# End keys and their transposes ahead, and key products on VectorE, in a gated linear attention

## The chip, the core and the metric

The program runs on one core of a Trainium2 chip. A core has five engines with queues of their own that run in order: TensorE (PE, matmuls; its weight loads are shown as PEld), VectorE (DVE), ScalarE (ACT), GpSimd (POOL) and SyncE (SP, here only DMA issues). The metric is the device time of one execution in microseconds, as the median of several runs.

## The reference

Two macaron layers of an encoder over 512 tokens and 16 meta tokens, width 1024, in float32. Each layer is half a feed-forward block, a mixer, and half a feed-forward block. The mixer adds a softmax attention and a gated linear attention (GLA) in both directions. The change lies in the GLA, with chunks and a decay `log_a` for each key channel:

```python
bcum = jnp.cumsum(log_a..., axis=3)      # inside a chunk
btot = bcum[:, :, :, -1:, :]
q_dec = qc * jnp.exp(bcum)
k_inv = kc * jnp.exp(-bcum)
k_end = kc * jnp.exp(btot - bcum)
att = jnp.where(mask, einsum('bhnid,bhnjd->bhnij', q_dec, k_inv), 0.0)
o_intra = einsum('bhnij,bhnjv->bhniv', att, vc)
kv_chunk = einsum('bhnjd,bhnjv->bhndv', k_end, vc)
# scan over chunks: S = exp(btot) * S + kv_chunk;  o_inter = q_dec @ S_prev
```

The backward direction is the same on the flipped sequence.

## The kernel before

All activations stand transposed, channels on 128 partitions and 528 tokens (512 and 16 meta tokens) along the row. A weight slab of 128x1024 is loaded by SP, split into a high part on ACT (L238, `whi`) and a low part on DVE (L239, `wlo`), and used in three matmuls per tile by `product` (L404); a projection's accumulator (`mm`) is evicted on DVE by `scaled` (L527) or on ACT (L691).

The GLA of a layer is two calls of `gla_pair` (L699), each for two heads, and each with the directions d = 0 (forward) and d = 1 (backward) in turn. The chunks are of 128 tokens, 4 blocks and the meta tokens. For one direction:

1. PE forms the gates z (L721). ACT takes abs, exp and log (L724 to L726), DVE finishes the log-sigmoid (L727) and scans it along each block (L731, five scans): `c` holds the sums.
2. DVE subtracts each block's middle value (`a`, L739 and L740) and its total (`ct_`, L741 and L742, a copy for the meta tokens). For d = 1 it first forms the reversed sums in `g` (L737).
3. ACT makes four exponentials (L746 to L749, or L752 to L755 for d = 1): for the queries, the keys, the state's queries and the end keys.
4. DVE multiplies the queries (`qp`, L757), POOL the keys (`kp`, L758), DVE the end keys (`ke`, L760). PE transposes the end keys (L764 for the blocks, L765 for the meta tokens), DVE copies them out (L767, L769), and makes the state's queries (L777) and copies the decays of blocks (L778).

After both directions PE forms the chunk states from the transposed end keys (L802), two banks `sm` taking turns; DVE chains them with the decays (L809, L817) and ACT copies the backward halves (L806, L813). The scores of queries and keys (L829), their mask (L832, L833) and the outputs (L837, L838) follow.

The order on each engine is not written out: a scheduler of the framework orders all instructions ahead of time by a priority that follows the order of the code, and fills in instructions of later code where it expects an engine to wait. So matmuls of later projections stand between the gates and the transposes on PE. `tc.high_priority()` lifts the instructions inside it over others that are ready. Tiles come from pools of fixed size by tag (`p` has 7, `t` has 6, the PSUM pairs `ss` 2).

Of the kernel before, what the change touches and what calls it, by code (L numbers as in the profile page):

```python
# [13 lines left out]
AF = mybir.ActivationFunctionType  # L14
ALU = mybir.AluOpType
AX = mybir.AxisListType

P = 128
# [3 lines left out]
META = 16  # L22
T = SEQ + META
# [249 lines left out]
def build(tc, ctx, xt, wts, win, par, w2, const, umask, out):  # L273
    nc = tc.nc
    V, S, G, TE = nc.vector, nc.scalar, nc.gpsimd, nc.tensor
# [30 lines left out]
    def nm(p):  # L306
        count[0] += 1
        return f"{p}{count[0]}"
# [3 lines left out]
    def slot(tag, dtype=F32, n=None):  # L312
        return slots[tag].tile([P, T], dtype, tag=tag, name=nm(tag))[:, : n or live[0]]
# [7 lines left out]
    def pair(second=False):  # L321
        return (slots["s2"] if second else pss).tile([P, 2, 512], F32, tag="s2" if second else "ss", name=nm("ss"))
# [22 lines left out]
    ident = ct[:, C_ID : C_ID + P]  # L345
# [7 lines left out]
    def v2(ap):  # L353
        return ap.rearrange("p (a b) -> p a b", a=2)
# [341 lines left out]
    blocks = [(b, slice(b * P, (b + 1) * P), P) for b in range(NB)]  # L696
    MB = slice(SEQ, T)

    def gla_pair(l, p, lr, w2t, sr, qa, ka, va, n_out):  # L699
# [6 lines left out]
        for hh in range(2):  # L706
            tp = pair()
# [6 lines left out]
        def blk(ap):  # L714
            return ap[:, :SEQ].rearrange("p (b t) -> p b t", b=NB)

        for d in range(2):
            z = pair()
            for i, hs in enumerate(halves):
                c0 = p * 256 + d * P  # L720
                TE.matmul(z[:, i, :HF], w2t[:, c0 : c0 + P], lr[:, hs], start=True, stop=True)  # L721
            a, g, c, ct_ = slot("t"), slot("t"), slot("t"), slot("t")

            S.activation(v2(a), z[:, :, :HF], AF.Abs)  # L724
            S.activation(a, a, AF.Exp, scale=-1.0)
            S.activation(a, a, AF.Ln, bias=1.0)  # L726
            V.scalar_tensor_tensor(v2(g), z[:, :, :HF], 0.0, v2(a), ALU.min, ALU.subtract)  # L727
            ones = ct[:, C_COS + SEQ : C_COS + SEQ + 1]
            for bs in [b[1] for b in blocks] + [MB]:
                n = bs.stop - bs.start  # L730
                V.tensor_tensor_scan(c[:, bs], ones.broadcast_to([P, n]), g[:, bs], 0.0, ALU.mult, ALU.add)  # L731
            mid = blk(c)[:, :, 63:64].broadcast_to([P, NB, P])
            tot = blk(c)[:, :, 127:128].broadcast_to([P, NB, P])
            mm_, mt_ = c[:, T - 1 : T].broadcast_to([P, META]), None
            src = c
            if d == 1:
                V.tensor_tensor(g, c, g, ALU.subtract)  # L737
                src = g
            V.tensor_tensor(blk(a), blk(src), mid, ALU.subtract)  # L739
            V.tensor_tensor(a[:, MB], src[:, MB], mm_, ALU.subtract)  # L740
            V.tensor_tensor(blk(ct_), blk(src), tot, ALU.subtract)  # L741
            V.tensor_copy(ct_[:, MB], a[:, MB])  # L742
            r16 = 1.0 / 16.0
            qp, kp = slot("p"), slot("p")
            if d == 0:
                S.activation(g, a, AF.Exp, scale=-r16)  # L746
                S.activation(a, a, AF.Exp, scale=r16)
                S.activation(c, c, AF.Exp, scale=r16)
                S.activation(ct_, ct_, AF.Exp, scale=-r16)  # L749
                ein, eq, ek, eend = c, a, g, ct_  # L750
            else:
                S.activation(c, a, AF.Exp, scale=-r16)  # L752
                S.activation(a, a, AF.Exp, scale=r16)
                S.activation(ct_, ct_, AF.Exp, scale=-r16)
                S.activation(g, g, AF.Exp, scale=r16)  # L755
                ein, eq, ek, eend = ct_, c, a, g
            V.tensor_tensor(qp[:, :n_out], qa, eq[:, :n_out], ALU.mult)  # L757
            G.tensor_tensor(kp, ka, ek, ALU.mult)  # L758
            ke = slot("p")
            V.tensor_tensor(ke, ka, eend, ALU.mult)  # L760

            tp = pair()
            for b, bs, _ in blocks:
                TE.transpose(tp[:, 0, bs], ke[:, bs], ident)  # L764
            TE.transpose(tp[:META, 1, :P], ke[:, MB], ident)  # L765
            for hh in range(2):
                V.tensor_copy(kt[hh][:, :SEQ].rearrange("p (b k) -> p b k", b=NB)[:, :, d * HD : (d + 1) * HD],  # L767
                              tp[:, 0].rearrange("p (b k) -> p b k", b=NB)[:, :, hh * HD : (hh + 1) * HD])
            V.tensor_copy(ktm[:META, 0:256].rearrange("p (h d k) -> p d h k", d=2, h=2)[:, d],  # L769
                          tp[:META, 1, :P].rearrange("p (h k) -> p h k", h=2))  # L770
            if qin is None:
                qin = [slot("p"), slot("p")]
            e0 = 127 if d == 0 else 0
            for hh in range(2):
                rows = slice(hh * HD, (hh + 1) * HD)
                to = slice(d * HD, (d + 1) * HD)
                V.tensor_tensor(qin[hh][to, :n_out], qa[rows], ein[rows, :n_out], ALU.mult)  # L777
                V.tensor_copy(dec[to, hh, :], blk(ein)[rows, :, e0])  # L778
            prods.append((qp, kp))
# [41 lines left out]
        for b in [3, 2, 1, 0] + [NB] * (n_out == T):  # L821
            bs, n = (MB, META) if b == NB else (blocks[b][1], P)
# [239 lines left out]
    def mixer(l, norm, done, following):  # L1062
# [15 lines left out]
        for p in range(2):  # L1078
            qa = project(x, rs, "i", 0.125, n_out)
            ka = project(x, rs, "i")  # L1080
            va = [project(x, rs, "i") for _ in range(2)]
            gla_pair(l, p, lr, w2t, sr, qa, ka, va, n_out)
# [115 lines left out]
    for l in range(DEPTH):  # L1198
        a, b, c = norms[3 * l : 3 * l + 3]
# [3 lines left out]
        if l < DEPTH - 1:  # L1203
            d = norms[3 * l + 3]
# [71 lines left out]
```

## Time and profile before

| | us |
|---|---|
| median of 3 runs | 2267.22 (2266.92 to 2269.97) |
| the profiled execution | 2263.49 |
| its span, first to last instruction | 2261.6 |
| PE busy | 2204.5 |
| DVE busy | 1527.2 |
| ACT busy | 1218.3 |
| POOL busy | 164.7 |

The four calls of `gla_pair` lie between about 427 and 524 us (layer 0) and between 1569 and 1656 us (layer 1). A row of a timeline reads: start, duration, engine, line and operation, output<-inputs, shapes, count, and in brackets the idle time of the engine just before and who ended it. A row of a wait reads: engine, what waited <- for whom: us in total, times, the longest. A row of windows reads: from:to, length, then the busy time of PE, PEld, DVE, ACT and POOL with the number of instructions, the granted PE clock, the share of the DMA engines and GB/s.

### The profile page before, as it was taken

The numbers are of one execution on the slowest core, as the hardware profiler recorded it, in microseconds if no ns is written. First come the engines' busy times: TensorE is split into PE (matmuls) and PEld (weight loads), VectorE is DVE, ScalarE is ACT, GpSimd is POOL, SyncE is SP. The second block draws the span as 40 slices with busy tenths as digits, with TensorE's granted clock in tenths as the row PEclk, the third lists the DMA queues.
The fourth block names the chain that finished last, engine by engine and source line by source line (L and its number), as shares of the span: only waits on it lengthen the run. The fifth ranks groups of instructions, "written<-read, shape, count | busy, mean of one in ns | idle before, by whom it ended". The sixth has DMA issues, their size and how long they took to land. (4 is left out here: it accounts for less than half of the span.)

```text
span 2261.6 us, 39885 instructions
## 1 busy us (share of the span) xinstructions
PE 2204.5 (97%) x16538; PEld 2102.9 (93%) x16538; DVE 1527.2 (68%) x2397; ACT 1218.3 (54%) x1824; POOL 164.7 (7%) x184
## 2 busy tenths in 40 slices
PE   8999999999999999999979999999999999999998
PEld 8999999989999999999979999998888888989897
DVE  7657567577876666565676565575789767756565
ACT  8536355344784564453565363454557836636354
POOL 1011000000000010101011010100000000101010
PEclk9999999999999999999999999999999999999999
DMA  8778463211113485867658585732121135869661
GB/s 239 188 177 212 134 168 108 75 57 57 48 38 113 124 203 154 197 174 173 180 139 207 139 217 149 178 105 87 56 68 54 47 121 152 215 155 225 156 181 66
DMA packets 87542, 312.85 MB, mean 138 GB/s; under 512 B 9664, under 2 KB 11840, under 8 KB 87360
## 3 DMA queue, kind: packets, MB, share of 16 engines
q1 hardware_dynamic: 60816, 217.67, 28.6%
q0 software_dynamic: 24768, 90.19, 22.5%
q8 instruction: 130, 2.13, 0.4%
q10 hardware_dynamic: 1776, 2.43, 0.3%
q14 instruction: 52, 0.43, 0.1%
HBM read 263.07 MB, written 2.10 MB: 117 GB/s over the span
## 5 line engine op out<-in xcount | busy, mean ns | idle before, releaser
L597 PE MATMUL ss<-xc,whi 128*128 128x264 f32 (+1 forms) x4720 | 865.1, 285 | 16.9 <-ACT whi L238 9.5
L597 PEld LDWEIGHTS ss<-xc,whi 128*128 128x128 f32 x4720 | 734.7, 189 | 19.7 <-ACT whi L238 10.3
L597 PE MATMUL ss<-xc,wlo 128*128 128x264 f32 (+1 forms) x2360 | 671.4, 285 | 5.1 <-DVE wlo L239 5.1
L404 PE MATMUL ss<-g,whi 128*128 128x264 f32 (+1 forms) x2620 | 482.8, 300 | 0.0
L597 PEld LDWEIGHTS ss<-xc,wlo 128*128 128x128 f32 x2360 | 446.8, 189 | 6.4 <-DVE wlo L239 6.3
L404 PEld LDWEIGHTS ss<-g,whi 128*128 128x128 f32 x2620 | 380.6, 188 | 15.7
L404 PE MATMUL mm<-x,whi 128*128 128x264 f32 (+1 forms) x1712 | 385.8, 315 | 0.0
L238 ACT CAST whi<-w 128x1024 fp32r<-128x1024 f32 (+1 forms) x220 | 230.0, 1046 | 266.2 <-PE ss L404 116.1
L239 DVE TENSOR_TENSOR wlo<-w,whi 128x1024 fp32r<-128x1024 f32 (+1 forms) x220 | 266.6, 1218 | 116.1 <-ACT whi L238 114.8
L238 ACT CAST whi<-raw 128x1024 fp32r<-128x1024 f32 x190 | 199.2, 1048 | 260.2 <-PE ss L597 89.8
L239 DVE TENSOR_TENSOR wlo<-raw,whi 128x1024 fp32r<-128x1024 f32 x190 | 232.1, 1222 | 105.8 <-ACT whi L238 104.8
L404 PE MATMUL ss<-g,wlo 128*128 128x264 f32 (+1 forms) x1310 | 302.2, 300 | 0.0
L404 PEld LDWEIGHTS mm<-x,whi 128*128 128x128 f32 x1712 | 281.2, 190 | 15.3 <-DVE x L393 0.2
L404 PE MATMUL mm<-x,wlo 128*128 128x264 f32 (+1 forms) x856 | 265.2, 314 | 0.0
L404 PEld LDWEIGHTS ss<-g,wlo 128*128 128x128 f32 x1310 | 209.2, 188 | 8.3
L239 DVE TENSOR_TENSOR wlo<-s,whi 128x1024 fp32r<-128x1024 f32 x86 | 105.1, 1222 | 95.7 <-ACT whi L238 95.6
L238 ACT CAST whi<-s 128x1024 fp32r<-128x1024 f32 x86 | 90.3, 1050 | 146.9 <-PE ss L597 128.3
L404 PEld LDWEIGHTS mm<-x,wlo 128*128 128x128 f32 x856 | 161.2, 190 | 7.6
L527 DVE SCALAR_TENSOR_TENSOR t<-ss,rs 128x528 f32<-128x528 f32 (+1 forms) x93 | 64.6, 700 | 126.4 <-PE ss L404 126.3
L189 ACT ACTIVATE s<-w 128x1024 f32<-128x1024 f32 x86 | 91.2, 1060 | 81.7 <-DMA w<-win 46.5
L194 POOL DMA_DIRECT2D w<-win x43 | 37.8, 880 | 599.3 <-DVE wlo L239 222.3
L393 DVE TENSOR_TENSOR g<-c,g 128x528 fp32r<-128x528 f32 (+1 forms) x88 | 61.5, 699 | 22.6 <-ACT g L392 22.6
(280 smaller groups left out, 2829.6 us busy)
## 6 DMA issues: line engine op xcount, KB each, us to landing
w<-win SPq DMA_DIRECT2D x218, 512.0 KB, 4.7
raw<-wts SPq DMA_DIRECT2D x190, 512.0 KB, 3.3
w<-win POOLq DMA_DIRECT2D x43, 512.0 KB, 6.8
s<-win POOLq DMA_DIRECT2D x43, 512.0 KB, 6.7
w<-s POOLq DMA_DIRECT2D x43, 512.0 KB, 5.9
s<-w POOLq DMA_DIRECT2D x43, 512.0 KB, 7.0
h<-xt SPq DMA_DIRECT2D x3, 528.0 KB, 7.6
out<-h SPq DMA_DIRECT2D x2, 512.0 KB, 2.9
```

Of the source, the lines that this page charges most:

```text
L189: self.nc.scalar.activation(t, w, AF.Copy, scale=-1.0)
L194: self.nc.gpsimd.dma_start(t, src, accum_op=ALU.add)
L238: nc.scalar.copy(hi[:, cs], w[:, cs])
L239: nc.vector.tensor_tensor(lo[:, cs], w[:, cs], hi[:, cs].bitcast(F32), ALU.subtract)
L393: V.tensor_tensor(lo, src, hi.bitcast(F32), ALU.subtract)
L404: TE.matmul(acc.half[i][:width], lhs, rhs[:, acc.spans[i]], start=first, stop=last)
L527: V.scalar_tensor_tensor(cut(dst[rows]), pv[rows], -0.5 * f, cut(rs[rows]), ALU.mult, ALU.mult)
L597: TE.matmul(acc[:, j], a[:, j, k], b[:, at], start=bool(begin and k == 0 and i == 0), stop=k == len(x) - 1 and i == 2, skip_group_check=no ...
```

## The change

Four edits, in both directions: the end-key chain (subtraction of totals, exponential, product) is written first after the scans and under high priority; the transposes of the end keys are written right behind it; the exponential goes straight into the tile `ke`, which is then multiplied in place; and the product of the keys, `kp`, moves from POOL to DVE. In the forward direction the meta tokens' copy becomes a subtraction. In the backward one, `ct_` (for the state's queries alone) is formed later. No arithmetic changes.

```diff
-            mm_, mt_ = c[:, T - 1 : T].broadcast_to([P, META]), None
+            last = c[:, T - 1 : T].broadcast_to([P, META])
+            r16 = 1.0 / 16.0
+            ke = slot("p")
             src = c
-            if d == 1:
-                V.tensor_tensor(g, c, g, ALU.subtract)
-                src = g
+            with tc.high_priority():
+                if d == 0:
+                    V.tensor_tensor(blk(ct_), blk(c), tot, ALU.subtract)
+                    V.tensor_tensor(ct_[:, MB], c[:, MB], last, ALU.subtract)
+                    S.activation(ke, ct_, AF.Exp, scale=-r16)
+                else:
+                    V.tensor_tensor(g, c, g, ALU.subtract)
+                    S.activation(ke, g, AF.Exp, scale=r16)
+                    src = g
+                V.tensor_tensor(ke, ka, ke, ALU.mult)
+            tp = pair()
+            for b, bs, _ in blocks:
+                TE.transpose(tp[:, 0, bs], ke[:, bs], ident)
+            TE.transpose(tp[:META, 1, :P], ke[:, MB], ident)
             V.tensor_tensor(blk(a), blk(src), mid, ALU.subtract)
-            V.tensor_tensor(a[:, MB], src[:, MB], mm_, ALU.subtract)
-            V.tensor_tensor(blk(ct_), blk(src), tot, ALU.subtract)
-            V.tensor_copy(ct_[:, MB], a[:, MB])
-            r16 = 1.0 / 16.0
+            V.tensor_tensor(a[:, MB], src[:, MB], last, ALU.subtract)
             qp, kp = slot("p"), slot("p")
             if d == 0:
...
-                S.activation(ct_, ct_, AF.Exp, scale=-r16)
-                ein, eq, ek, eend = c, a, g, ct_
+                ein, eq, ek = c, a, g
             else:
+                V.tensor_tensor(blk(ct_), blk(src), tot, ALU.subtract)
+                V.tensor_copy(ct_[:, MB], a[:, MB])
...
-                S.activation(g, g, AF.Exp, scale=r16)
-                ein, eq, ek, eend = ct_, c, a, g
+                ein, eq, ek = ct_, c, a
             V.tensor_tensor(qp[:, :n_out], qa, eq[:, :n_out], ALU.mult)
-            G.tensor_tensor(kp, ka, ek, ALU.mult)
-            ke = slot("p")
-            V.tensor_tensor(ke, ka, eend, ALU.mult)
-
-            tp = pair()
-            for b, bs, _ in blocks:
-                TE.transpose(tp[:, 0, bs], ke[:, bs], ident)
-            TE.transpose(tp[:META, 1, :P], ke[:, MB], ident)
+            V.tensor_tensor(kp, ka, ek, ALU.mult)
```

New lines of the changed kernel that are named below: L740, L741 and L744 the subtractions, L742 and L745 the exponential and L747 the product of the end key, L750 and L751 its transposes, L767 and L768 the products of queries and keys, L770 and L772 the copies out, L780 the state's queries, L781 the decays, L805 the state products, L812 their chain.

What the scheduler makes of it, on DVE in layer 0, first call, forward direction, behind the scans (`t_4917` is `c`, `t_4918` is `ct_`, `t_4915` is `a`; `wlo` is a weight split; L527 evicts a projection):

```order
-L739 TENSOR_TENSOR t_4915<-t_4917 128x512
-L740 TENSOR_TENSOR t_4915<-t_4917 128x16
-L741 TENSOR_TENSOR t_4918<-t_4917 128x512
-L742 COPY t_4918<-t_4915 128x16
+L740 TENSOR_TENSOR t_4918<-t_4917 128x512
+L741 TENSOR_TENSOR t_4918<-t_4917 128x16
 L239 TENSOR_TENSOR wlo_5151<-raw_4779,whi_5150 128x1024
-L778 COPY dec_4890<-t_4917 64x4 x2
-L757 TENSOR_TENSOR p_4932<-i_4654,t_4915 128x528
-L760 TENSOR_TENSOR p_4940<-i_4713,t_4918 128x528
+L747 TENSOR_TENSOR p_4928<-i_4713,p_4928 128x528
+L781 COPY dec_4890<-t_4917 64x4 x2
```

The end-key product stands right behind the weight split; the decay copies and the query product, which stood ahead of it, come after it.

The same queue in the backward direction, before (`t_4961` is `g`, `t_4963` is `ct_`):

```order
L737 TENSOR_TENSOR t_4961<-t_4962,t_4961 128x528
L739 TENSOR_TENSOR t_4960<-t_4961,t_4962 128x512
L741 TENSOR_TENSOR t_4963<-t_4961,t_4962 128x512
L757 TENSOR_TENSOR p_4978<-i_4654,t_4962 128x528
L777 TENSOR_TENSOR p_4951<-i_4654,t_4963 64x528
L760 TENSOR_TENSOR p_4986<-i_4713,t_4961 128x528
```

and now:

```order
L744 TENSOR_TENSOR t_4961<-t_4962,t_4961 128x528
L752 TENSOR_TENSOR t_4960<-t_4961,t_4962 128x512
L747 TENSOR_TENSOR p_4973<-i_4713,p_4973 128x528
L761 TENSOR_TENSOR t_4963<-t_4961,t_4962 128x512
L767 TENSOR_TENSOR p_4985<-i_4654,t_4962 128x528
L768 TENSOR_TENSOR p_4986<-i_4713,t_4960 128x528
L780 TENSOR_TENSOR p_4951<-i_4654,t_4963 64x528
L812 SCALAR_TENSOR_TENSOR q_5001<-q_5001,dec_4890,sm_5010 64x128 x2
```

The end-key product moves ahead of the query product and of the subtraction of totals; the query and key products (L767, L768) now stand behind it and ahead of the first state update (L812).

On PE, the projection matmuls (L404) between the gates and the transposes become fewer. In layer 0 there were 73 and 87 in the first call (forward, backward) and are 66 and 69, and in the second 80 and 91 and are 66 and 81; in layer 1 there were 50 and 97, and 40 and 62, and are 35 and 79, and 40 and 38. Behind the backward transposes of the first call stands now:

```order
L750 MATMUL ss_4977<-const,p_4973 128x128 x4
L751 MATMUL ss_4977<-const,p_4973 16x128
L832 MATMUL ss_5041<-p_4941,p_4942 128x128 x2
L404 MATMUL mm_5267<-x_4202,wlo_4776 128x264
...
L805 MATMUL sm_5006<-k_4895 128x128 x2
L805 MATMUL sm_5010<-q_4893,q_4891 128x128
L805 MATMUL sm_5010<-q_4894,q_4892 128x128
L832 MATMUL ss_5056<-p_4941,p_4942 128x128
L805 MATMUL sm_5016<-q_4893,q_4891 128x128
L805 MATMUL sm_5016<-q_4894,q_4892 128x128
L832 MATMUL ss_5041<-p_4985,p_4986 128x128 x2
```

The scores of the backward direction (from `p_4985` and `p_4986`), which stood beside those of the forward one right behind the transposes, now come after three pairs of state products. SP's queue keeps its order, and POOL's loses the eight products L758 and nothing else.

## The prediction

> **What bounds the kernel now.** I read the page first, then the waits of TensorE (PE), then the timeline of the four passes of the linear attention, engine by engine.
>
> ```profile
> PE 2204.5 (97%) x16538; PEld 2102.9 (93%) x16538; DVE 1527.2 (68%) x2397; ACT 1218.3 (54%) x1824; POOL 164.7 (7%) x184
> PE ss L764 <- DVE p L760: 12.5, 8, 2.1
> PE ss L597 <- ACT whi L238: 9.5, 4, 4.7
> ```
>
> PE is busy for 97% of the span, and the change adds and takes away none of its work. So the end moves only by PE's idle time and by its clock. The largest wait of PE is the one that the change is about: eight times (two layers, two passes, two directions) the transposes of the end keys (L764) wait for the DVE product that makes them (L760), 12.5 us in all. The next row belongs to the feed-forward part, which the change leaves alone. The eight places, with the idle time before each in brackets:
>
> ```profile
> 439.77 0.63 PE L764 MATMUL ss<-const,p 128*128 128x128 f32 x4 [1.46 <-DVE p L760]
> 453.47 0.30 PE L764 MATMUL ss<-const,p 128*128 128x128 f32 x1 [2.13 <-DVE p L760]
> 492.67 0.34 PE L764 MATMUL ss<-const,p 128*128 128x128 f32 x1 [1.83 <-DVE p L760]
> 507.80 0.41 PE L764 MATMUL ss<-const,p 128*128 128x128 f32 x2 [1.49 <-DVE p L760]
> 1581.13 0.41 PE L764 MATMUL ss<-const,p 128*128 128x128 f32 x2 [1.43 <-DVE p L760]
> 1595.25 0.41 PE L764 MATMUL ss<-const,p 128*128 128x128 f32 x2 [1.31 <-DVE p L760]
> 1629.30 0.41 PE L764 MATMUL ss<-const,p 128*128 128x128 f32 x2 [1.11 <-DVE p L760]
> 1642.57 0.41 PE L764 MATMUL ss<-const,p 128*128 128x128 f32 x2 [1.75 <-DVE p L760]
> ```
>
> A wait is the length of a chain (gates, scans, exponentials, product) less the projection matmuls that stand ahead of the transposes on PE and cover it. The change shortens both, so each must be counted.
>
> **The first place, forward direction.** DVE's queue from the end of the scans, with ACT's exponential and POOL's key product beside it:
>
> ```profile
> 433.94 0.69 DVE L739 TENSOR_TENSOR t<-t 128x512 f32<-128x512 f32 x1
> 434.55 0.17 DVE L740 TENSOR_TENSOR t<-t 128x16 f32<-128x16 f32 x1
> ...
> 435.66 1.22 DVE L239 TENSOR_TENSOR wlo<-raw,whi 128x1024 fp32r<-128x1024 f32 x1
> 436.79 1.48 DVE L778 COPY dec<-t 64x4 f32<-64x4 f32 x2
> 438.30 0.71 DVE L757 TENSOR_TENSOR p<-i,t 128x528 f32<-128x528 f32 x1
> 438.93 0.70 DVE L760 TENSOR_TENSOR p<-i,t 128x528 f32<-128x528 f32 x1
> ```
>
> ```profile
> 435.15 0.64 ACT L746 ACTIVATE t<-t 128x528 f32<-128x528 f32 x1
> 435.88 2.19 POOL L758 TENSOR_TENSOR p<-i,t 128x528 f32<-128x528 f32 x1 [122.50 <-ACT t L746]
> 450.91 1.85 POOL L758 TENSOR_TENSOR p<-i,t 128x528 f32<-128x528 f32 x1 [12.84 <-DVE i L527]
> ```
>
> The new order keeps four subtractions, a projection's eviction and the weight split L239 ahead of the end-key product. Behind L239, at 436.79, it now stands at once: the two decay copies (1.51 us to the next start) and the query product (0.63) are behind it. The exponential (0.64) runs while DVE is at the split. The chain is shorter by 2.14. For the cover, the order has 66 matmuls between the gate product and the transposes where 73 were. Their price:
>
> ```profile
> 440.60:451.30 10.70, 10.70 (x89) 10.53 (x87) 8.93 (x21) 5.45 (x10) 0.39 (x1) 1.00 0.14 49
> 1619.10:1628.10 9.00, 9.00 (x40) 7.03 (x38) 7.54 (x16) 6.48 (x11) 1.60 (x1) 1.00 0.27 88
> 1630.30:1640.80 10.50, 10.50 (x62) 9.11 (x61) 9.64 (x21) 7.21 (x12) 0.67 (x1) 1.00 0.18 60
> ```
>
> The first row holds 87 weight loads in 10.70 us, 0.123 us a matmul of 264 columns; the second 40 of 512 columns, 0.225 each. Seven matmuls are 0.86 us, and the wait becomes 1.46 - 2.14 + 0.86 = 0.18.
>
> **The first place, backward direction.** Rows of DVE and ACT:
>
> ```profile
> 443.23 0.71 DVE L727 SCALAR_TENSOR_TENSOR t<-ss,t 128x528 f32<-128x528 f32 x1 [1.02 <-ACT t L726]
> ...
> 446.67 0.70 DVE L737 TENSOR_TENSOR t<-t,t 128x528 f32<-128x528 f32 x1
> ...
> 451.61 1.72 DVE L760 TENSOR_TENSOR p<-i,t 128x528 f32<-128x528 f32 x1
> 453.36 0.16 DVE L778 COPY dec<-t 64x4 f32<-64x4 f32 x1
> ```
>
> ```profile
> 440.80 0.61 ACT L724 ACTIVATE t<-ss 128x528 f32<-128x528 f32 x1 [3.40 <-PE ss L721]
> 442.55 0.65 ACT L726 ACTIVATE t<-t 128x528 f32<-128x528 f32 x1
> ```
>
> Before, 12.7 us pass from the end of the gate product (440.76, just ahead of L724) to the transposes at 453.47. After: the forward products, the key product among them, now fill DVE until 0.5 us past ACT's logarithm, so L727 begins 2.97 after the gate product, where it was 2.47. Then L727 to the scans and L239 take 3.44 as before (443.23 to 446.67), the subtraction, an eviction and one more subtraction 1.56, the product 0.70, the way to PE 0.14: 8.8 in all, 3.9 shorter. The cover falls from 87 to 69 matmuls, 2.2 us. The wait becomes 2.13 - 3.9 + 2.2 = 0.43.
>
> The same walk at the other six, chain shorter by / cover smaller by / wait left: second pass 2.7 / 1.7 / 0.86 and 10.4 us of chain against 81 matmuls or 10.0 / 0.4; layer 1, 2.8 / 1.8 / 0.46 (15 matmuls), 3.1 / 2.2 / 0.40 (18), 0.7 / 0 / 0.39, 3.15 / 1.9 / 0.50 (62 matmuls in 10.5 become 38 of 512 columns). Sum of the eight: 3.7. **The waits give 12.5 - 3.7 = 8.8 us.** Unsure is each place by some 0.5 us, as three of the eight products stand right behind a weight split that needs ACT: the ends are 0 and 1.1 us left per place (0 to 9 us), and I keep 3.7, since it comes from the nearest rows.
>
> **The key product on DVE.** POOL's eight go (1.35 to 2.19 us each). A DVE product of this size takes 0.70 (L757); eight are 5.0 us of DVE at a distance of 0.63, counted above where they delay the backward chain. What goes with POOL is larger: the rows of 435.88 and 450.91 lie over a DVE instruction that ends only after POOL does. The two copies at 436.79 take 1.48, where one takes 0.16 (453.36); L760 at 451.61 takes 1.72 instead of 0.70. Each place has one such instruction, all ahead of L760 or L760 itself; they add 0.64 to 1.14 us, 8.1 us together. The last:
>
> ```profile
> 1641.08 1.34 DVE L760 TENSOR_TENSOR p<-i,t 128x528 f32<-128x528 f32 x1
> ```
>
> That is part of the shorter chains, not added to them.
>
> **Behind the backward transposes.** The backward query and key products now stand behind them on DVE, and the state updates (L812, was L809) behind these. Queued from the end-key product to the first update: two subtractions, three copies, two full products, an eviction, two half products and two copies.
>
> ```profile
> 440.55 0.76 DVE L767 COPY q<-ss 128x256 f32<-128x256 f32 x2
> L777 DVE TENSOR_TENSOR p<-i,t x16: 674/694/1731, 439.9 to 1642.6; 64x528 f32<-64x528 f32 x8, 64x512 f32<-64x512 f32 x8
> 1595.92 0.71 PE L829 MATMUL ss<-p,p 64*128 64x128 f32 x8
> 1598.01 0.71 PE L802 MATMUL sm<-q,q 128*128 128x128 f32 x4
> ```
>
> That is 0.63 + 0.77 + 0.95 + 0.62 + 0.35 + 0.62 + 1.7 = 5.6 us; the first update and ACT's copy of the bank add 0.9, and the start lies 0.84 ahead of the transposes, so the bank that PE reuses is due 5.7 after these begin. PE meanwhile has the transposes 0.6, eight score products 1.3 (the L829 row is four, in two records each), 14 to 21 projection matmuls 1.7 to 2.8 and three pairs of state products of 0.64: 5.5 to 6.6. The margin is -0.2 to 0.9, and I charge 0.5 us for the four passes; a DVE later by 1 us would cost about 0.6 at each, 2.4 us, and a gain is excluded because PE showed no wait there.
>
> **The clock.** Windows of 3.41 us around two of the waits, one in layer 1, and one in the softmax attention (PEclk is the third number from the end):
>
> ```profile
> 451.84:455.25 3.41, 1.78 (x16) 1.47 (x17) 3.34 (x5) 0.46 (x1) 0.92 (x1) 1.00 0.02 5
> 455.25:458.66 3.41, 3.41 (x17) 3.17 (x16) 2.36 (x7) 0.00 (x0) 0.00 (x0) 0.50 0.49 154
> 489.38:492.80 3.42, 1.59 (x14) 1.41 (x13) 3.38 (x6) 1.20 (x3) 1.58 (x1) 1.00 0.44 153
> 492.80:496.21 3.41, 3.41 (x17) 3.33 (x17) 2.69 (x6) 1.78 (x4) 0.00 (x0) 0.50 0.00 0
> 1639.68:1643.09 3.41, 1.66 (x15) 1.41 (x13) 3.30 (x6) 0.86 (x2) 1.73 (x1) 1.00 0.48 154
> 578.13:581.54 3.41, 3.41 (x18) 3.26 (x17) 2.11 (x7) 1.44 (x4) 0.00 (x0) 0.50 0.00 0
> ```
>
> Behind the two longest waits of layer 0 the granted clock was half for 3.41 us, which costs 1.7 us each. With waits under 0.9 us PE is busy for at least 2.5 of such a window, so I take both as gone: **3.4 us**. The ends are 0 (the wait of 1.75 in layer 1 was not followed by half clock, and at 578 half clock came with no wait) and 5 (that one goes too). [...]
>
> **Sum.** 8.8 - 0.5 + 3.4 = 11.7 us. The profiled execution took 2263.49 (span 2261.6), so it would take 2251.8; the median of the runs shown is 2267.22, 3.7 above, so the forecast of the median is **2255.5**.
>
> **The rivals.**
> - *The clock does not hang on these waits.* Only 8.3 goes: 2258.9. For it: 578 and 1639.68 above. Chance 0.2.
> - *The change does not bring the product forward in fact.* 49 matmuls of layer 0 (6.0 us) and some 6 us in layer 1 are taken off the cover; if the weight splits and exponentials ahead of the product come late, 1.1 us is left per place: 8.8 left, 3.7 gained, 2263.5. For it: such small excesses over a plan are what the 4.4 us of today's waits are that POOL does not explain (12.5 - 8.1). Chance 0.17.
> - *Slower: the stretch belongs to DVE's products and not to POOL.* Then 8.1 us stays in the chains while the cover is gone: 3.7 + 8.1 = 11.8 left; the products added ahead of the backward chains and of the updates stretch too (1 us at eight places, 8 us), and half clock follows in four places rather than two (3.4 more): 11.8 - 12.5 + 8 + 3.4 = 10.7 lost, 2278. It decides from about 1.2 us a product instead of 0.7. Against it: L757, the same shape, takes 0.71 where POOL rests, and the stretched ones end with POOL's or behind. Chance 0.05.
>
> The forecast has the remaining 0.58. The low end of the range takes all of the waits and 5 us of clock: 2267.2 - 17.5, rounded to 2249; the high end takes in the second rival: 2264. Faster by over 0.2% (about what a measurement of this kernel can tell from no change, 4.5 us) is the forecast and the first rival and a little of the second, 0.8; within 0.2%, 0.15; slower, 0.05.
>
> **What would show it.** Right: the wait of PE on the end-key product at 3 to 5 us for eight; no DVE instruction of 1.2 us or more among products and decay copies; PEclk at 1.00 from 427 to 524; no new PE wait on the state products (L805) over 0.3 us. Wrong: waits near 1 us each (the second rival), L767 and L768 over 1 us (the third), or half clock in these passes without a wait (the first).

## The result, and the profile after

The changed kernel took 2249.78 us (median of 4 runs, 2247.43 to 2250.33), the kernel before 2267.07 (4 runs, 2262.35 to 2269.97). The ratio is 0.9924, interval 0.9905 to 0.9942: 17.3 us less. The forecast was 2255.5, in a range of 2249 to 2264, so the median lies 0.8 us inside the fast end of the range. The profiled execution of the changed kernel took 2247.43 us, its span 2245.5.

The first part of its page, with busy time, share of the span and instructions of each engine:

```profile
PE 2199.3 (98%) x16538; PEld 2098.8 (93%) x16538; DVE 1520.4 (68%) x2405; ACT 1217.7 (54%) x1824; POOL 150.9 (7%) x176
```

PE does the same 16538 matmuls. DVE has eight instructions more, 5.6 us of products, and is less busy all the same (1520.4 for 1527.2): others on DVE became shorter. The waits of PE in the changed kernel that belong to the linear attention (us in total, times, the longest):

```profile
PE ss L750 <- DVE t L753: 1.9, 4, 0.6
PE ss L750 <- DVE p L747: 1.5, 4, 0.5
...
PE sm L840 <- DVE t L836: 0.6, 2, 0.4
```

The first two rows are one wait, that of the transposes on the end-key product: `t L753` is a short subtraction behind the product, to which four of the eight are put down. Together 3.4 us, where 12.5 stood. No row on the state products (L805) of any size has come in their place. The eight places in the timeline of PE:

```profile
435.25 0.63 PE L750 MATMUL ss<-const,p 128*128 128x128 f32 x4 [0.20 <-DVE p L747]
445.11 0.63 PE L750 MATMUL ss<-const,p 128*128 128x128 f32 x4 [0.46 <-DVE t L753]
480.64 0.63 PE L750 MATMUL ss<-const,p 128*128 128x128 f32 x4 [0.53 <-DVE p L747]
492.06 0.63 PE L750 MATMUL ss<-const,p 128*128 128x128 f32 x4 [0.57 <-DVE t L753]
1565.81 0.63 PE L750 MATMUL ss<-const,p 128*128 128x128 f32 x4 [0.47 <-DVE t L753]
1576.77 0.63 PE L750 MATMUL ss<-const,p 128*128 128x128 f32 x4 [0.36 <-DVE t L753]
1610.71 0.63 PE L750 MATMUL ss<-const,p 128*128 128x128 f32 x4 [0.31 <-DVE p L747]
1620.86 0.63 PE L750 MATMUL ss<-const,p 128*128 128x128 f32 x4 [0.42 <-DVE p L747]
```

And DVE's queue at the first of them:

```profile
433.28 1.22 DVE L239 TENSOR_TENSOR wlo<-raw,whi 128x1024 fp32r<-128x1024 f32 x1
434.41 0.70 DVE L747 TENSOR_TENSOR p<-i,p 128x528 f32<-128x528 f32 x1
435.03 0.34 DVE L781 COPY dec<-t 64x4 f32<-64x4 f32 x2
435.38 0.71 DVE L767 TENSOR_TENSOR p<-i,t 128x528 f32<-128x528 f32 x1
436.00 0.70 DVE L768 TENSOR_TENSOR p<-i,t 128x528 f32<-128x528 f32 x1
```

The end-key product stands right behind the weight split and takes 0.70; the two decay copies take 0.34 together, where they took 1.48; the key product, now on DVE (L768), takes 0.70.

The clock over the four passes of layer 0, by the windows of before and of after (PEclk is the third number from the end):

```profile
427.00:524.00 97.00, 89.79 (x697) 83.51 (x696) 71.13 (x153) 45.35 (x98) 8.02 (x4) 0.96 0.15 50
```

```profile
427.00:524.00 97.00, 94.89 (x766) 88.67 (x765) 75.06 (x169) 51.85 (x108) 0.00 (x0) 1.00 0.18 58
```

The half clock behind two of the waits is gone, and in 97 us PE is busy 5.1 us more, with 766 matmul records where 697 stood.

**Where the 17 us went.** A mixer is measured here from its first low-rank matmul (L1051, after L1054) to the first feed-forward matmul (L580) behind its attention, by their starts in the trace. Layer 0 went from 390.9 to 379.9 us, layer 1 from 360.0 to 356.5: 14.4 us in both. The profiled executions differ by 16.1; the other 1.7 lies in code that did not change, and the medians' further 1.2 between the runs.

### The profile page after: what moved, and what is told of

It is laid out like the page before. It is cut to its first block, busy times and chain, and to the rows that moved or that the text cites. A ratio compares the mean times of both kernels' runs of the same rounds, so it can differ in the third digit from the quotient of the medians.

```text
span 2245.5 us, 39862 instructions
## 1 busy us (share of the span) xinstructions
PE 2199.3 (98%) x16538; PEld 2098.8 (93%) x16538; DVE 1520.4 (68%) x2405; ACT 1217.7 (54%) x1824; POOL 150.9 (7%) x176
## 5 line engine op out<-in xcount | busy, mean ns | idle before, releaser
L404 PE MATMUL ss<-g,whi 128*128 128x264 f32 (+1 forms) x2620 | 482.8, 300 | 0.0
L404 PEld LDWEIGHTS ss<-g,whi 128*128 128x128 f32 x2620 | 380.6, 188 | 15.8
L404 PE MATMUL mm<-x,whi 128*128 128x264 f32 (+1 forms) x1712 | 384.2, 313 | 0.0
L239 DVE TENSOR_TENSOR wlo<-w,whi 128x1024 fp32r<-128x1024 f32 (+1 forms) x220 | 266.5, 1218 | 117.9 <-ACT whi L238 116.5
L239 DVE TENSOR_TENSOR wlo<-raw,whi 128x1024 fp32r<-128x1024 f32 x190 | 232.1, 1222 | 104.1 <-ACT whi L238 101.1
L404 PE MATMUL ss<-g,wlo 128*128 128x264 f32 (+1 forms) x1310 | 302.2, 300 | 0.0
L404 PEld LDWEIGHTS mm<-x,whi 128*128 128x128 f32 x1712 | 279.3, 188 | 15.4 <-DVE x L393 0.2
L404 PE MATMUL mm<-x,wlo 128*128 128x264 f32 (+1 forms) x856 | 265.3, 315 | 0.0
L404 PEld LDWEIGHTS ss<-g,wlo 128*128 128x128 f32 x1310 | 209.3, 188 | 8.3
L239 DVE TENSOR_TENSOR wlo<-s,whi 128x1024 fp32r<-128x1024 f32 x86 | 105.1, 1222 | 92.9 <-ACT whi L238 92.9
L404 PEld LDWEIGHTS mm<-x,wlo 128*128 128x128 f32 x856 | 159.8, 189 | 8.0
L527 DVE SCALAR_TENSOR_TENSOR t<-ss,rs 128x528 f32<-128x528 f32 (+1 forms) x93 | 64.6, 699 | 126.0 <-PE ss L404 125.9
```

The source lines that it names most:

```text
L239: nc.vector.tensor_tensor(lo[:, cs], w[:, cs], hi[:, cs].bitcast(F32), ALU.subtract)
L404: TE.matmul(acc.half[i][:width], lhs, rhs[:, acc.spans[i]], start=first, stop=last)
L527: V.scalar_tensor_tensor(cut(dst[rows]), pv[rows], -0.5 * f, cut(rs[rows]), ALU.mult, ALU.mult)
```

## The experiments

Two explanations fit the result. **The hold**: POOL's key product holds up the DVE instruction beside it, so that moving it is what shortens the chains. **The order**: the end keys come sooner since they are written first, and the move hardly matters. Beside these stands the clock: does half clock hang on these waits, or come and go with the execution?

| kernel | ratio to before, interval | end-key waits, layer 0 / 1 | mixer, layer 0 / 1 | PEclk 427 to 524 |
|---|---|---|---|---|
| before | | 6.9 / 5.6 | 390.9 / 360.0 | 0.96 |
| before_again | | 7.6 / 5.6 | 396.0 / 360.0 | 0.91 |
| before_third | | 7.7 / 5.6 | 390.0 / 360.0 | 0.98 |
| kp_l1 | 0.9987 [0.9975, 0.9999] | 7.7 / 2.0 | 394.5 / 356.4 | 0.93 |
| kp_l0 | 0.9957 [0.9940, 0.9973] | 2.8 / 5.6 | 383.5 / 360.0 | 1.00 |
| kp_only | 0.9934 [0.9913, 0.9956] | 2.8 / 2.1 | 382.1 / 356.5 | 1.00 |
| order_only | 0.9963 [0.9948, 0.9977] | 3.6 / 2.4 | 383.4 / 357.7 | 1.00 |
| pool_beside | 0.9950 [0.9936, 0.9964] | 3.6 / 3.6 | 381.9 / 358.4 | 1.00 |
| after | 0.9924 [0.9905, 0.9942] | 1.8 / 1.6 | 379.9 / 356.5 | 1.00 |
| after_again | 0.9931 [0.9907, 0.9954] | 1.8 / 1.6 | 380.0 / 356.5 | 1.00 |

Waits are the idle times before the four transposes of a layer, summed from the timeline; all in us.

### kp_only: the engine alone

```diff
-            G.tensor_tensor(kp, ka, ek, ALU.mult)
+            V.tensor_tensor(kp, ka, ek, ALU.mult)
```

This is the kernel before with that one line.

> The kernel before with one edit: the key product kp on DVE instead of POOL; its scheduled order puts it ahead of the end-key product, and the cover on PE grows by 8, 6, 5, 2, 8, -7, -1 and 6 matmuls. Theory (POOL's product stretches a DVE instruction in each chain, which the scheduler does not foresee; the order of the chain matters little, because the scheduler sizes the cover to it): no DVE instruction over 1.2 us among products and decay copies, PE's wait on the end keys 3 to 6 us instead of 12.5, ratio to before 0.993 to 0.996. Rival (the earlier end key brings the gain): the chain is 0.6 us longer at each place, PE's wait 12 to 17 us, ratio 0.999 to 1.003.

It took 2252.45 us (6 runs), ratio 0.9934. The wait of PE, and the groups of DVE's instructions (busy us, mean ns; those of L758 are the key product itself):

```profile
PE ss L764 <- DVE p L760: 4.9, 8, 1.0
```

```profile
L777 DVE TENSOR_TENSOR p<-i,t 64x528 f32<-64x528 f32 (+1 forms) x16 | 11.1, 693 | 0.2
L758 DVE TENSOR_TENSOR p<-i,t 128x528 f32<-128x528 f32 x8 | 5.6, 704 | 0.0
L760 DVE TENSOR_TENSOR p<-i,t 128x528 f32<-128x528 f32 x8 | 5.6, 701 | 0.0
...
L778 DVE COPY dec<-t 64x4 f32<-64x4 f32 x16 | 2.6, 160 | 0.2
L742 DVE COPY t<-t 128x16 f32<-128x16 f32 x8 | 1.3, 168 | 0.0
```

The same groups in the kernel before:

```profile
L777 DVE TENSOR_TENSOR p<-i,t 64x528 f32<-64x528 f32 (+1 forms) x16 | 12.1, 758 | 0.2
L760 DVE TENSOR_TENSOR p<-i,t 128x528 f32<-128x528 f32 x8 | 7.3, 909 | 0.1
L778 DVE COPY dec<-t 64x4 f32<-64x4 f32 x16 | 7.0, 438 | 0.2
...
L742 DVE COPY t<-t 128x16 f32<-128x16 f32 x8 | 2.3, 290 | 0.0
```

With the key product away from POOL the four groups lose 1.0 + 1.7 + 4.4 + 1.0 = 8.1 us, and the wait of PE 12.5 - 4.9 = 7.6. A mean that mixes held instructions with free ones looks harmless (438 ns for L778, of which four of sixteen are held); the timeline shows single ones of 1.3 us. The engine alone gives most of the gain: 12.3 us of the mixers' 14.4, in both against the first profile of before.

### order_only: the order alone

The changed kernel with the key product back on POOL:

```diff
-            V.tensor_tensor(kp, ka, ek, ALU.mult)
+            G.tensor_tensor(kp, ka, ek, ALU.mult)
```

> The changed kernel with the key product back on POOL: the new order of the end-key chain alone. Theory (POOL's product is the cause): one DVE instruction per place is again 0.6 to 1.1 us too long, now behind the forward end-key product, so that the four forward waits stay near 0.4 us and the four backward ones are 1 to 2 us, with 0 to 3 us of new waits at the state products; PE's waits there 6 to 11 us, ratio to before 0.996 to 1.000. Rival (order): waits of 3 to 4 us as in the changed kernel, ratio 0.992 to 0.995.

It took 2259.67 us (12 runs), ratio 0.9963. The first place on POOL and DVE, from the timeline:

```profile
435.43 1.65 POOL L768 TENSOR_TENSOR p<-i,t 128x528 f32<-128x528 f32 x1 [121.99 <-ACT t L756]
...
434.69 1.21 DVE L239 TENSOR_TENSOR wlo<-raw,whi 128x1024 fp32r<-128x1024 f32 x1
435.82 1.81 DVE L747 TENSOR_TENSOR p<-i,p 128x528 f32<-128x528 f32 x1
437.56 0.33 DVE L781 COPY dec<-t 64x4 f32<-64x4 f32 x2
```

The product is first in the queue as the change wants it, and yet takes 1.81, since POOL's began 0.4 us before it. At the other seven places POOL's product now falls behind the end-key product, on a decay copy, a query product or the state's queries, so the transposes wait less than before (6.0 us in all). The expectation had this only in part: the first forward wait is 1.31 us and not 0.4, and two of the four backward ones stay at 0.5. So the order has a worth of its own, 9.8 us of the mixers against 12.3 for the engine; the two overlap, since either takes the longest waits away and the half clock with them. What the order adds to the engine is 2.1 us of the mixers (after against kp_only); the medians cannot tell that much apart.

### after_again and before_again: the scatter

> The changed kernel, unaltered, on this chip. Theory: ratio 0.991 to 0.995, PE's wait on the end keys 3 to 4 us, no half clock between 427 and 524 us. For the clock: if half clock in the softmax attention (578 us before) depends on the GLA's waits, none there again; if it comes by chance, it may.

The changed kernel once more took 2253.20 (6 runs, 2248.62 to 2255.83), ratio 0.9931: 3.4 us above its first median, with mixers of the same length to 0.1 us and, as expected, no half clock between 427 and 600. The two profiled executions (2247.43 and 2255.83) differ by 8.4 us; their stretches of half clock, 24.6 and 40.3 us in all and none of them in a mixer, explain 7.9 of it.

> The kernel before, unaltered, profiled once more. Theory (half clock follows the two longest waits): half clock of 3.41 us again behind at least one of the waits near 452 and 492 us. Rival (half clock comes by chance of the phase of its windows): at other places, or none there; and the half clock at 62 and 578 us may come or go. PE's wait on the end keys 12 to 13 us either way.

The kernel before took 2270.90 in a single run; 17 runs of it beside these kernels had a median of 2267.26. Layer 1's mixer repeats to 0.03 us and the waits to 0.8, but layer 0's mixer is 5 us longer than in the first profile, nearly all of it by half clock: it starts at 454.58, 509.19 and 584.28, the second for 13.7 us. So one of the two waits named had half clock again; the other had none, and a third one, of 2.23 us at 507, had it.

### kp_l0 and kp_l1: one layer at a time

```diff
-            G.tensor_tensor(kp, ka, ek, ALU.mult)
+            (V if l == 0 else G).tensor_tensor(kp, ka, ek, ALU.mult)
```

and `l == 1` for the other; both on the kernel before.

> The kernel before, with the key product on VectorE in layer 0 alone. Theory (a POOL product holds up the DVE instruction beside it; what the wait grows by brings half clock in layer 0): PE waits on the end keys in layer 0 fall from 6.9 to about 2.5 us, in layer 1 they stay at 5.6; no half-clock window in the attention part of layer 0; layer 0's mixer (first low-rank matmul to first feed-forward matmul) about 382 us instead of 391 to 396, layer 1's 360; ratio about 0.995. Rival (half clock comes and goes with the execution, whatever POOL does): half clock again near 455 or 580, mixer of layer 0 at 386 or more, ratio 0.998.

> The kernel before, with the key product on VectorE in layer 1 alone. Theory: layer 1's waits fall from 5.6 to about 2.4 and its mixer from 360.0 to 356.5 us; layer 0 keeps waits of 6.9, a half-clock window near 455 and one near 580, mixer 391 to 396; ratio about 0.9985, 3.5 us. Rival (half clock comes and goes with the execution): layer 0 without half clock, mixer about 385, though its waits stay.

kp_l0 took 2256.19 (6 runs), ratio 0.9957, kp_l1 2263.72 (12 runs), ratio 0.9987; before 2266.77 (17 runs). The layers separate cleanly: the mixer of the layer that was changed has the length of kp_only to 1.4 us, the other that of before. By the ratios layer 0 is worth 10 us and layer 1 three, for waits that lose 4.1 and 3.6 us. The difference is clock. A window of kp_l0 over the four passes of layer 0, and one in its softmax attention:

```profile
427.00:524.00 97.00, 94.14 (x751) 87.97 (x750) 72.91 (x163) 49.70 (x105) 0.00 (x0) 1.00 0.17 55
570.30:573.70 3.40, 3.40 (x18) 3.25 (x17) 2.64 (x9) 1.94 (x5) 0.00 (x0) 0.50 0.00 0
```

and of kp_l1:

```profile
427.00:524.00 97.00, 89.10 (x668) 82.18 (x668) 68.78 (x148) 43.26 (x92) 8.04 (x4) 0.93 0.15 50
507.54:521.20 13.66, 13.66 (x57) 11.40 (x58) 7.09 (x22) 2.17 (x7) 0.00 (x0) 0.50 0.00 0
```

Both expectations missed a part. kp_l1 has its half clock behind the fourth wait of layer 0 (507.54, four times as long as a usual stretch) and none behind the second. kp_l0 has one in the softmax attention at 570.30, though its waits are short.

### pool_beside: POOL's work put back, for nothing

The changed kernel with one product more on POOL, in the forward direction, whose output nothing reads; the key product stays on VectorE.

```diff
                     S.activation(ke, ct_, AF.Exp, scale=-r16)
+                    G.tensor_tensor(ct_, ka, ct_, ALU.mult)
```

> The changed kernel, with an added POOL product of end-key size (the keys by the tile of the subtracted totals, which nothing reads afterwards) at the four forward places, released by the same exponential as the end-key product; no result uses it. Theory (POOL holds up the DVE instruction beside it): at the four forward places the DVE instruction that runs beside POOL takes 1.2 to 1.8 us instead of 0.70, and the PE wait there grows from 0.2 to 0.5 to about 1 to 1.5 us, 3 to 4 us in all; the backward places stay under 0.6; ratio to before about 0.995 without half clock, 0.997 with it. Rival (the gain is one of DVE's order, and POOL's work is harmless as such): waits and DVE durations as in the changed kernel, 0.992 to 0.993.

It took 2255.94 (6 runs), ratio 0.9950. Its lines stand one lower than in the changed kernel (L748 is the end-key product, L751 its transposes). The first pass, then the second, from the timeline:

```profile
438.41 2.19 POOL L743 TENSOR_TENSOR t<-i,t 128x528 f32<-128x528 f32 x1 [120.83 <-ACT p L742]
...
438.21 1.22 DVE L239 TENSOR_TENSOR wlo<-raw,whi 128x1024 fp32r<-128x1024 f32 x1
439.35 1.82 DVE L748 TENSOR_TENSOR p<-i,p 128x528 f32<-128x528 f32 x1
...
441.31 0.63 PE L751 MATMUL ss<-const,p 128*128 128x128 f32 x4 [1.32 <-DVE p L748]
...
485.90 1.83 POOL L743 TENSOR_TENSOR t<-i,t 128x528 f32<-128x528 f32 x1 [45.30 <-ACT p L742]
...
485.86 0.71 DVE L748 TENSOR_TENSOR p<-i,p 128x528 f32<-128x528 f32 x1
486.79 2.03 DVE L239 TENSOR_TENSOR wlo<-raw,whi 128x1024 fp32r<-128x1024 f32 x1 [0.23 <-ACT whi L238]
...
498.85 0.63 PE L751 MATMUL ss<-const,p 128*128 128x128 f32 x4 [1.26 <-DVE t L754]
```

In the first pass the end-key product starts behind POOL's and takes 1.82 instead of 0.70; the wait of PE grows from 0.20 to 1.32. In the second pass the end-key product starts 0.04 us ahead of POOL's and is not held: the weight split behind it is (2.03 for 1.22), and the bill comes at the backward transposes, 1.26 for 0.57. So one of the four places went otherwise than expected, by the same mechanism. In layer 1 both forward waits grow (1.32 for 0.47, 1.43 for 0.31). The four add 3.8 us, and the two mixers are longer by 3.8. An instruction whose result is thrown away costs this much. So the rival falls in its claim that POOL's work is harmless; that the order is worth something too was seen in order_only.

### before_third

> The kernel before, unchanged, a third profile. Theory: PE waits on the end keys 12 to 13.5 us; half clock near 455 and again in the softmax attention of layer 0 (578 to 590), as in both profiles of it. Rival (half clock comes and goes with the execution): one of the two is missing.

A single run, 2264.09 us: waits of 13.3, half clock at 456.87 and 579.75, 3.4 us each, as expected.

### Two edits without effect

Two of the four edits do nothing here. Without `tc.high_priority()`, or with the transposes written where they stood before, the scheduled order of all five engines is that of the changed kernel row for row, so there was nothing to run. What moves the end-key product forward is that its subtraction, exponential and product are written first.

## Why the prediction was right, and where its size was off

**PE's waits are the bound: right.** The mixers' 14.4 us are the waits (12.5 to 3.3, 9.2 us by the rows of the timeline) and some 5 us of clock. No other wait took their place.

**The waits, 8.8 us: 9.2.** Seven of the eight places came within 0.2 us of the working (0.18, 0.43, 0.4 and 0.46, 0.40, 0.39, 0.50 predicted, 0.20, 0.46, 0.57 and 0.47, 0.36, 0.31, 0.42 found); the third was put at 0.86 and is 0.53. (The eight as listed add to 3.6, where the prediction has 3.7.) Counting both the chain and the cover was needed: a chain that is 2.1 us shorter gained only 1.26, since the order has seven matmuls fewer ahead of the transposes.

**The key product and POOL, 8.1 us inside the chains: shown.** kp_only takes the 8.1 us off DVE by the engine alone, pool_beside brings the hold back with a product that has no use, order_only shows it on the product that the change had just moved to the front. What was argued from pairs of rows is now shown by putting the cause in and taking it out. The traces also show what the order of the starts does: at 485.86 of pool_beside the product ahead of POOL's by 0.04 us keeps its length (0.71), at 435.82 of order_only the one behind by 0.39 takes 1.81. The rival in which the stretch belongs to DVE's own products is refuted by L768, eight times 0.70 us.

**The second rival, that the product would not come forward: wrong.** No place keeps 1.1 us, as it had it.

**Behind the backward transposes, 0.5 us lost: not more.** No wait on the state products came. In layer 1, where no half clock disturbs the sum, the waits shrank by 4.0 us and the mixer by 3.5, so up to 0.6 us went elsewhere; which instruction has it was not found.

**The clock, 3.4 us: mis-sized; the profiles show about 5.** This is the term that was off. The first profile lost three stretches between 427 and 600, not two: at 455.25, 492.80 and 578.13, at about 1.7 us each, and after has none of them. The two that the working charged are there, 3.4 us; it had the third as its upper end. What the stretches behind the waits cost (half their length) varies: 3.4, 8.5 and 1.7 us in the three profiles of before and 6.8 in kp_l1, 5.1 on the mean. So does layer 0's mixer, which took 390.9, 396.0 and 390.0 in these three and 394.5 in kp_l1, on the mean 392.9, but 379.9 and 380.0 in the two of the changed kernel. The first profile of before, on which the sum was made, is one of the shorter ones.

**The first rival, that the clock does not hang on these waits: wrong for the passes; the stretch in the softmax attention has another cause.** In the ten profiles there are eighty such waits. Of seven of 2.09 us or more, five were followed by half clock within 2 us; of four of 1.83, one; of 69 of 1.76 or less, none. The four profiles whose layer 0 is that of before have all of them; POOL's work as such does not do it, as order_only and pool_beside show a clock of 1.00 with POOL's products in these passes.

The traces also show why one wait pays and the next does not. In each profile all stretches of half clock start on one grid with a step of 3.413 us, which lies differently in each execution. Cut at this grid, the ten profiles hold 6162 windows of full clock between 100 and 2230 us. All 27 in which PE is busy for less than 1.6 us are followed by half clock, 13 of the 20 with 1.6 to 1.85 us, and five of the 6115 with more. So a wait of about 2 us can pay when it falls into one window. The two long ones that were not followed are parted by the grid: the wait of 2.09 us that ends at 454.03 in kp_l1, and the one of 2.23 that ends at 508.87 in before_third (the number behind the length is PE's busy time):

```profile
449.52:452.93 3.41, 2.41 (x20) 2.20 (x18) 2.64 (x6) 3.18 (x5) 1.45 (x1) 1.00 0.16 65
452.93:456.34 3.41, 2.31 (x21) 2.00 (x22) 3.34 (x6) 0.00 (x0) 0.38 (x1) 1.00 0.02 5
```

```profile
504.66:508.07 3.41, 1.98 (x17) 1.77 (x15) 3.37 (x5) 1.97 (x4) 1.80 (x1) 1.00 0.45 147
508.07:511.48 3.41, 2.61 (x22) 2.16 (x22) 3.32 (x9) 0.00 (x0) 0.00 (x0) 1.00 0.04 12
```

In both profiles of the changed kernel every such window between 427 and 524 has PE busy for 2.8 us or more. In the first profile of before, the windows ahead of the two stretches behind its longest waits have 1.78 (451.84) and 1.59 (489.38).

The five windows with more than 1.85 us are those ahead of the stretches in the softmax attention (578 to 584 in the four profiles with the old layer 0, 570.30 in kp_l0), with PE at work all the time. Each of the five holds a whole group of small matmuls, sixteen of two columns (L915) and four of sixteen (L917). In the first profile:

```profile
575.44 1.02 PE L915 MATMUL ss<-const,t 128*128 128x2 f32 x8
577.00 0.95 PE L915 MATMUL ss<-const,t 128*128 128x2 f32 x8
```

Without this group PE is busy for 1.6 us of each of the five. In the other five profiles the grid parts the group, 1.7 us or more are left in each window, and no half clock follows. So in the ten profiles this stretch goes with where the group falls on the grid, and not with a wait of the linear attention. That the small matmuls themselves bring it on was not shown, as no run alters them; and why all four profiles with the old layer 0 have the stretch, and only one of the six others, was not found.

**The median.** 2255.5 against 2249.78 is 5.7 us: 2.7 of it in the mixers (14.4 for 11.7: 1.7 is clock, 0.4 the waits, and 0.5 the charge behind the transposes, which the sum of both layers does not show), the other three outside them, where two medians of the same changed kernel differ by 3.4.

## What to carry to other kernels

An elementwise product on POOL was not free beside the busy DVE of this kernel: each of 128x528 cost one DVE instruction 0.3 to 1.15 us, which the schedule did not foresee, and the same product on DVE cost 0.70. Look for it as single instructions of an unusual length with a POOL span beside them, by shape and not by the group's mean. Where an engine waits for a chain, count the cover that the schedule takes away along with the chain, and price a wait by the clock behind it too: by the ratios of kp_l0 and kp_l1, layer 0's 4.1 us of waits were worth 10 us, layer 1's 3.6 only 3.

## What the runs showed of the hardware

- Each of the 44 POOL products of 128x528, in the seven profiles that have them, held one DVE instruction, the next to start whose operands all lie in SBUF. In before the end-key product took 1.72 at 451.61 for 0.70, and even a copy of 64x4 (0.16 us, L778) took 1.27 at 505.64. An eviction, which reads a PSUM bank, passed: at 1640.73 of before L527 took its 0.43 beside POOL's product of 1640.13, and the end-key product behind it was the one held (1.34).

```profile
1640.73 0.43 DVE L527 SCALAR_TENSOR_TENSOR i<-mm,rs 128x264 f32<-128x264 f32 x1
1641.08 1.34 DVE L760 TENSOR_TENSOR p<-i,t 128x528 f32<-128x528 f32 x1
```

- The hold went both ways. POOL's product took 1.3 to 2.2 us, and ended 1.16 to 1.18 after the end of the DVE instruction that was running when it started (438.41, 485.90 and 1616.48 of pool_beside; L239, L748 and L239 beside them). Where that instruction was an eviction (L527), it took 1.33 (1571.34 of pool_beside) and 1.35 (1577.26 of before).
- In each of the ten profiles half clock started on a grid of 3.413 us and lasted 3.41 us or a multiple of it (13.65 in two profiles; the stretch that runs into the end of the program is cut off there). It followed every window of the grid in which PE was busy for less than 1.6 us (27), some of those with 1.6 to 1.82, and none with more, apart from the five with the small matmuls. Why some stretches last for two to four windows was not found.
